# Decay blocks by a subtraction on GpSimd and one exponential, and two more gate blocks by seven products in the front

## The chip, the core and the metric

The kernel runs on one core of a Trainium2 chip. A core has a matrix engine (TensorE, PE in the profile; its weight loads are the row PEld), a vector engine (VectorE, DVE), a scalar engine for functions such as the exponential (ScalarE, ACT), GpSimd (POOL) and a sync engine (SP) that here issues nearly all DMA transfers. Each engine has its own instructions, in the order in which the program was written, and waits on semaphores for the others. The metric is the time of one execution on the device in microseconds (us).

## What is computed

One layer of a decoder on 1024 tokens of width 1024, in float32. One wide projection feeds two token mixers, and gates merge them:

```python
h = rms_norm(x, norm_w)
q, k, v, z_a, xbc, z_s, dt_raw, gate_logits = split(h @ w_in)
y_a = diff_attention(q, k, v) * silu(z_a)            # 8 heads, two softmax maps each
y_s = ssd_chunked(conv(xbc), softplus(dt_raw + dt_bias), -exp(a_log))   # 32 heads, 4 groups
y_s = gated_group_rms_norm(y_s, z_s)
merged = sigmoid(g_a) * (y_a @ w_proj_attn) + sigmoid(g_s) * (y_s @ w_proj_ssd)
out = x + merged @ w_out
```

The gate logits have 2048 columns, 16 blocks of 128: blocks 0 to 7 are g_a, 8 to 15 are g_s. In the chunked scan (8 chunks of 128 tokens) the decay of a head within a chunk is

```python
seg = a_t[..., :, None] - a_t[..., None, :]          # a_t: cumulative sum of dt * A in the chunk
decay = exp(where(causal, seg, -inf))                # 128 x 128 for each head
```

and multiplies the products of C and B before they meet x.

## The kernel before, in words

**Three-part products.** Float32 factors are split into a rounded high part and the rest, and a product is three matmuls: high by high, high by rest, rest by high (`steps3`). `hH` and `hL` are the two parts of h, 16 slices of 128 x 1024 together.

**Two ways for a block of the projection.** Directly, a block of 128 output columns is two halves of 512 tokens, each 8 row blocks of three matmuls (`gates`, `proj_half`): 48 matmuls of 512 columns. Or two neighbouring blocks, four quarters of a product, go together by seven products instead of eight (Strassen-like, `front_pair`): each of the seven takes a sum or difference of weight quarters (`pair_splits`, sums on GpSimd) and a form of h, which is a quarter or a sum of quarters of it. That is 7 x 4 x 3 = 84 matmuls for the pair, with additions behind them (`front_sum`, `gate_step`). The forms t1 to t4 of h are kept in 16 big buffers while the front lasts (`form_tiles`).

**Stages.** `bulk` writes TensorE's main stream, in this order:

1. the front: `FRONT_ORDER`, a list written out by hand. `y` and `e` are the first products of the z columns and of gate blocks 0, 2, 4 and 6 before all forms are there; `c` is a pair of convolution blocks, `g` a pair of gate blocks, `z06` and the like one of seven products of the z columns, `d` the dt columns. `FRONT` is 12: the front does gate blocks 0 to 11;
2. the eight attention heads' projections (`att_proj`, tile `pma`);
3. `gates`: the gate blocks from `FRONT` to 15, directly (tile `pg`). The second half of block 15 is the last use of h and frees its slices one by one for other data;
4. `products(0)`, `products(1)`, `products(2)`: the products of the two branches with their projections, each by seven products in two passes over pairs of output blocks (tiles `px`, `py`, `pz`); then `final`, the output product.

**What runs between.** Scan chunks (`ssd_core`, `ssd_chunk`), attention blocks (`att_core`, `att_block`), the sums of forms (`sums_of`), the loads and splits of forms for the products (`fill`, `get_form`) and those of weights (`w_loads`, `w_splits`) are tasks. While the program is built, a planner (`Plan`) keeps a clock for each engine with a cost for each instruction, and puts a task's next instructions into the stream when their inputs are due; otherwise the main stream goes on. So the order on every engine is fixed when the kernel is built; on the chip only the waits decide.

**Buffers around the change.** Of the big pool (17 buffers of 4 KB a partition) the forms of h hold 16 during the front. In the heads a head holds 4 (`v`, `zg`, two `kk`), a half of its queries 1, an attention block of the second half 2 (`p`), a decay block 1 (`abb`, one at a time). The products read forms too, 7 forms of 4 tiles for each of the three: `get_form` takes a slice pair of h if one is free, else a big buffer, and leaves three big buffers for others until attention and scan are done. A form is loaded, then copied on ACT and its rest taken on DVE (`split_form`). `products` uses the 28 tiles in the order `ORDER` in its first pass and gives them back in its second; b22 comes last in it.

**A decay block** (`load_ab`): the cumulative sums of 8 heads of a chunk are loaded to all partitions as 128 x 8 x 128, GpSimd's affine_select puts -1e30 where the key comes after the query, and ACT takes the exponential of each head's 128 x 128 with the bias `nac`, the negative cumulative sum of the partition: 8 instructions. Then DVE multiplies by `pc` (C times B), and TensorE uses the block in small matmuls (tiles `pD`, `pO`).

Of the kernel before, what the change touches and what calls it, by code (L numbers as in the profile page):

```python
# [11 lines left out]
AF = mybir.ActivationFunctionType  # L12
ALU = mybir.AluOpType
AX = mybir.AxisListType

P = 128
# [6 lines left out]
GH = 8  # L23
# [9 lines left out]
C_GATE = 9248  # L33
NBIG, NW, NRAW, NMID, NSM = 17, 9, 4, 16, 8
PACE = 17.5
FRONT = 12
SLOW = 32.0
FRONT_ORDER = "y0 e4 y1 e0 g8 c6 d0 c20 z06 c16 z07 c10 g0 c2 z05 z04 c0 z16 g6 z03 g2 z17 c4 z15 z13 z14 c8 c14 g4 c12 g10 c18 c22"
REST = (("t2", 6), ("b22", 3), ("t3", 7), ("t1", 5), ("t4", 4))
ZSUMS = (83.0, 185.0, 9.0)  # L40
WPOOL = 2
# [4 lines left out]
HOP = 0.12  # L46
# [107 lines left out]
def tile_hybrid_layer(ctx: ExitStack, tc: tile.TileContext, x, norm_w, w_in, q_norm_w, k_norm_w,  # L154
# [37 lines left out]
    def bigt(shape, dt=F32, name="b"):  # L192
        return big.tile(shape, dt, tag="b4", name=name)

    def midt(shape=(P, 512), dt=F32, name="m"):
        return mid.tile(list(shape), dt, tag="b2", name=name)
# [47 lines left out]
    def in_ps(*aps):  # L244
        return any(a.space == bass.MemoryType.PSUM for a in aps)
# [3 lines left out]
    def act(o, i, f, after, **kw):  # L249
        nc.scalar.activation(o, i, f, **kw)  # L250
        if f in (AF.Silu, AF.Exp) and f != table[0]:
            table[0] = f
            pl.op("A", 1.3, after)
        c = 0.83e-3 * i.free_size() + (0.052 if in_ps(i) else 0.093) + 0.093 * (("accum_out" in kw) + any(not isinstance(kw.get(i, 0.0), float) for i in ("scale", "bias")))
        return pl.op("A", c, after)

    def tt(o, a, b, op, after, eng="V"):
        (nc.vector if eng == "V" else nc.gpsimd).tensor_tensor(out=o, in0=a, in1=b, op=op)  # L258
        n = o.free_size()
        if eng == "G":  # L260
            return pl.op("G", 0.095 + (1.85e-3 if op == ALU.mult else 2.3e-3) * n, after, True)
        sb = not in_ps(a, b)
        return pl.op("V", 0.07 + 0.07 * sb + 1.042e-3 * n, after, sb)
# [14 lines left out]
    def load(o, i, after=0.0):  # L278
        nc.sync.dma_start(out=o, in_=i)
        q = pl.op("Q", 0.48, max(after, pl.t))  # L280
        n = o.free_size() * 512 / 360e3 if o.space != bass.MemoryType.DRAM else i.free_size() * 512 / 360e3
        return pl.op("D", n, q + 0.6) + lag[1]
# [83 lines left out]
    def block_w(src, nkb, c0, cols=P):  # L366
        return [(src[q * 512:(q + 1) * 512, c0:c0 + cols].rearrange("(k p) c -> p k c", p=P), 4, cols)
                for q in range(nkb // 4)]
# [5 lines left out]
    ORDER1 = []  # L374
    for e in FRONT_ORDER.split():
        ORDER1.append((e[0], int(e[1:])))
# [32 lines left out]
    NFRONT = len(wlist)  # L409
    for ob in range(FRONT, 16):  # L410
        wlist += block_w(w_in, KB, C_GATE + ob * P)
# [187 lines left out]
    def w_next(n):  # L599
        i = used[0]  # L600
        used[0] += n
        return list(range(i, i + n))
# [202 lines left out]
    def att_proj(h):  # L805
# [10 lines left out]
        for ts in ((0, 1), (2,), (3,), (4,), (5,), (6,), (7,)):  # L816
            pms = []
            for t in ts:
                k = yield from pl.get(trs, first=True)
                pms.append((mmt(f"pma{h}{t}"), k))  # L820
                if t % 2 == 0:
                    km = yield from pl.get(qkm)
                    qk.append([midt([P, 2, 256], name=f"qk{h}{t}"), km, 0])
            if FRONT == 16 and h == HEADS - 1 and ts[0] == NT - 1:
                pl.spawn(h_done())
# [12 lines left out]
    def h_done():  # L838
        yield pl.t + 5.6
        for k in range(2 * KB):  # L840
            hs.give(k, pl.t)
# [215 lines left out]
    nac = const.tile([P, NT, SH], F32, name="nac")  # L1057
# [435 lines left out]
    def ssd_core(g):  # L1493
        state = {"st": {}, "pre": {}, "n": 0, "did": set()}
        ssd_n[g] = state
        abs_ = {}

        def load_ab(c):
            k = yield from pl.get(abb)
            ab = bigt([P, GH, P], name=f"ab{g}{c}")  # L1500
            t = load(ab, act_d[c, g * GH:(g + 1) * GH, :].partition_broadcast(P)) + 1.0
            yield t
            nc.gpsimd.affine_select(out=ab, in_=ab, pattern=[[0, GH], [1, P]], compare_op=ALU.is_ge, fill=-1e30,  # L1503
                                    base=0, channel_multiplier=-1)
            t = pl.op("G", 1.06, t, True)
            yield t
            for j in range(GH):
                t = act(ab[:, j, :], ab[:, j, :], AF.Exp, t - HOP, bias=nac[:, c, g * GH + j:g * GH + j + 1])
            abs_[c] = (ab, k, t)
        need = [(b, h) for b in [16 + g, 20 + g] + list(range(g * 4, g * 4 + 4)) for h in range(2)]  # L1510
        while any(cv_at.get(i, INF) > pl.t for i in need) or any(z_at.get((g, t), INF) > pl.t for t in range(NT)):
            yield pl.t + 0.5
        pl.spawn(load_ab(0))
        for c in range(NT):
            if c + 1 < NT:
                pl.spawn(load_ab(c + 1))
            while c - state["n"] >= 2 or c and c - 1 not in state["did"]:
                yield pl.t + 0.2
            pl.spawn(ssd_chunk(g, c, state, abs_))
            yield pl.t + (PACE if bigs.avail(3) <= pl.t or 'setup' in ready else SLOW)  # L1520
# [181 lines left out]
    def gates():  # L1702
        for ob in range(FRONT, 16):
            ids = w_next(2)
            for n in range(2):
                k = yield from pl.get(trs, first=True)
                pm = mmt(f"pg{ob}{n}")
                yield from proj_half(pm, ids, n, n == 1, ob == 15 and n == 1)
                pl.spawn(gate_evac(ob, n, pm, k), pe_done())
# [541 lines left out]
```

## Time and profile before

| | us |
|---|---|
| median of 3 runs | 1552.48 |
| lowest, highest | 1551.68, 1552.88 |
| the profiled execution | 1552.03 |
| its span, first to last instruction | 1550.0 |
| first of the decay blocks' loads | 327.2 |
| last of the decay blocks' matmuls | 1069.6 |
| first, last matmul of the direct gate blocks (`pg`, 192) | 1179.6, 1236.6 |

How to read it: the page gives busy times and shares of the engines, the groups of instructions that cost most (mean ns of one, and the idle time of their engine before them), and the chain of waits that ended last, followed back from the end. The chain in order of time, the timeline and the windows show single stretches. Names such as `pg` are tiles of the program, written "out<-in". Ends of matmuls are modelled: one of 512 columns shows some 400 ns though the next begins about 227 ns after it, so starts are compared rather than lengths.

### The profile page before, as it was taken

Reading aid. Unit: us, or ns where it says so; the run is one execution under the profiler, and the core shown is the slowest. Engines: PE = TensorE matmul, PEld = TensorE weight load, DVE = VectorE, ACT = ScalarE, POOL = GpSimd, SP = SyncE. Lnnn points to the kernel's source line nnn. Section 1 sums busy time; section 2 is a strip of 40 time slices with the busy share of each in tenths; the row PEclk is TensorE's granted clock in tenths of the full one; section 3 lists DMA queues with packets and bytes.
Section 4 is the critical chain, followed back from the end, with each engine's and each line's share of the span. In section 5 each row is a group of like instructions: output and inputs, shape, how many; then the busy total and the mean of one; then the engine's idle time right before and its main releaser. Section 6 shows DMA issues by size and latency. Waiting matters only on the chain.

```text
span 1550.0 us, 26098 instructions
## 1 busy us (share of the span) xinstructions
PE 1534.9 (99%) x8562; PEld 1253.3 (81%) x8562; DVE 1131.5 (73%) x2091; ACT 887.6 (57%) x2203; POOL 806.9 (52%) x922
## 2 busy tenths in 40 slices
PE   7999999999999999999999999999999999999999
PEld 5887888888888878787878887888878888888887
DVE  6757978657688776877677777777456687888985
ACT  8654434355666666767766776766556555352350
POOL 3276376544555545455685645574768754322005
PEclk9999999999999999999999999999999999999999
DMA  7576678666544472324463424152438679698836
GB/s 237 172 222 215 218 254 292 205 200 224 187 143 130 133 215 77 117 77 143 153 204 117 150 76 135 62 174 82 157 137 264 228 275 315 227 333 262 308 130 224
DMA packets 255977, 289.56 MB, mean 187 GB/s; under 512 B 18519, under 2 KB 162656, under 8 KB 255842
## 3 DMA queue, kind: packets, MB, share of 16 engines
q1 hardware_dynamic: 255838, 287.89, 57.4%
q8 instruction: 68, 1.11, 0.3%
q14 instruction: 67, 0.55, 0.1%
q10 hardware_dynamic: 4, 0.00, 0.0%
HBM read 198.57 MB, written 89.26 MB: 186 GB/s over the span
## 4 chain that ended last, share of the span: by engine, by line
PE 91%; POOL 2%; DVE 2%; ACT 2%; DMA 2%; issue 1%; SPq 0%; POOLq 0%; DVEq 0%; ACTq 0%
PE pma L218 21%; PE pz L218 11%; PE fYc L218 6%; PE py L218 5%; PE fXc L218 4%; PE sc L218 4%; PE fZc L218 4%; PE av L218 4%; PE fYg L218 3%; PE px L218 3%; PE pO L218 3%; PE pg L218 3%; PE pmz L218 2%; PE pa L233 2%; PE poz L218 1%; PE fZg L218 1%
## 5 line engine op out<-in xcount | busy, mean ns | idle before, releaser
L218 PE MATMUL pma<-w,hH 128*128 128x512 f32 x1024 | 347.4, 407 | 0.6 <-ACT at L250 0.6
L218 PEld LDWEIGHTS pma<-w,hH 128*128 128x128 f32 x1024 | 186.9, 188 | 40.6 <-issue 5.5
L218 PE MATMUL pma<-w,hL 128*128 128x512 f32 x512 | 208.4, 407 | 0.0
L250 ACT ACTIVATE w<-raw 128x512 fp32r<-128x512 f32 (+1 forms) x166 | 102.5, 630 | 65.3 <-DMA raw<-wf_d 25.1
L218 PEld LDWEIGHTS pma<-w,hL 128*128 128x128 f32 x512 | 96.6, 189 | 20.0 <-issue 3.0
L258 POOL TENSOR_TENSOR rawf<-rawf,rawf 128x512 f32<-128x512 f32 x54 | 70.6, 1307 | 79.8 <-DVE wp L258 37.2
L258 DVE TENSOR_TENSOR w<-raw,w 128x512 fp32r<-128x512 f32 (+1 forms) x114 | 91.0, 810 | 23.8 <-ACT w L250 23.6
L250 ACT ACTIVATE p<-p,nm 128x256 f32<-128x256 f32 (+7 forms) x128 | 98.2, 769 | 17.1 <-DVE nm L946 13.8
L218 PE MATMUL fYc<-ft,wp 128*128 128x512 f32 x432 | 105.6, 391 | 0.0
L218 PEld LDWEIGHTS fYc<-ft,wp 128*128 128x128 f32 x432 | 80.6, 188 | 16.7
L258 POOL TENSOR_TENSOR w<-raw,w 128x512 fp32r<-128x512 f32 x52 | 69.9, 1350 | 41.2 <-ACT w L250 41.2
L218 PE MATMUL pz<-w,ft 128*128 128x512 f32 x384 | 91.3, 392 | 0.0
L250 ACT ACTIVATE wp<-rawp 128x512 fp32r<-128x512 f32 x72 | 44.5, 628 | 76.6 <-POOL rawp L258 18.2
L258 POOL TENSOR_TENSOR rawp<-rawp,rawp 128x512 f32<-128x512 f32 x36 | 52.7, 1469 | 59.8 <-DVE wp L258 50.8
L218 PEld LDWEIGHTS pz<-w,ft 128*128 128x128 f32 x384 | 71.5, 188 | 14.7
L250 ACT ACTIVATE ab<-ab,nac 128x128 f32<-128x128 f32 x256 | 78.4, 395 | 2.2 <-POOL ab L1503 1.7
L946 DVE CUSTOM_DVE_ANT_0 p<-sc,maskb 128x512 f32<-128x512 f32 (+3 forms) x128 | 69.1, 585 | 13.5 <-PE sc L218 13.3
L218 PEld LDWEIGHTS av<-v,at 128*128 128x128 f32 x576 | 73.3, 191 | 4.5 <-issue 0.4
L290 POOL TENSOR_TENSOR rs<-rs,mhalf 128x4 f32<-128x4 f32 (+1 forms) x71 | 73.1, 1030 | 5.9
L258 POOL TENSOR_TENSOR os<-os,os 128x512 f32<-128x512 f32 x48 | 68.9, 1436 | 13.4 <-DMA os<-in_w_in_dram 5.4
L218 PE MATMUL av<-v,at 128*128 128x128 f32 x576 | 75.4, 275 | 0.0
L250 ACT ACTIVATE wp<-rawf 128x512 fp32r<-128x512 f32 x100 | 60.1, 624 | 23.0 <-POOL rawf L258 20.6
(376 smaller groups left out, 4171.1 us busy)
## 6 DMA issues: line engine op xcount, KB each, us to landing
raw<-in_w_in_dram SPq DMA_DIRECT2D x104, 256.0 KB, 3.2
rawf<-in_w_in_dram SPq DMA_DIRECT2D x72, 256.0 KB, 3.8
ab<-act_d SPq DMA_DIRECT2D x32, 512.0 KB, 5.3
wf_d<-os SPq DMA_DIRECT2D x48, 256.0 KB, 2.3
cv_d<-cv SPq DMA_DIRECT2D x48, 256.0 KB, 2.5
raw<-wf_d SPq DMA_DIRECT2D x48, 256.0 KB, 3.2
t_d<-ts SPq DMA_DIRECT2D x24, 512.0 KB, 2.7
os<-in_w_in_dram SPq DMA_DIRECT2D x32, 256.0 KB, 5.2
```

What stands on the lines that cost most here:

```text
L218: nc.tensor.matmul(o, lhsT=lhsT, rhs=rhs, start=start, stop=stop, **kw)
L233: nc.tensor.transpose(out=o, in_=i, identity=ident if idn is None else idn)
L250: nc.scalar.activation(o, i, f, **kw)
L258: (nc.vector if eng == "V" else nc.gpsimd).tensor_tensor(out=o, in0=a, in1=b, op=op)
L290: nc.gpsimd.tensor_tensor(out=dst, in0=dst, in1=mhalf[:, 0:cols], op=ALU.pow)
L946: nc.vector.tensor_tensor_reduce(out=p[:, j:e], in0=sc[m][:, o:o + e - j], in1=maskb[:, S - n + j:S - n + e], scale=-1.0, scalar=nms[i - 1 ...
```

## The change

Three things are changed. Gate blocks 12 and 13 move from the direct way behind the heads to a pair by seven products in the front (`FRONT` 14, `g12` in the list); `gates` keeps blocks 14 and 15. The front's list has a new order: `z07` stands before `c16`, `c14` where `c4` was and `c4` behind `z15`, and `g12` behind `c12`. And in a decay block GpSimd adds `nac` to all eight heads at once, with `nac` repeated along the columns, and one exponential on ACT takes the whole block. That is the subtraction of the reference's `seg`, as `nac` is negative. The cost that the planner puts down for both is that of its helpers `tt` and `act`.

```diff
-FRONT = 12
+FRONT = 14
 SLOW = 32.0
-FRONT_ORDER = "y0 e4 y1 e0 g8 c6 d0 c20 z06 c16 z07 c10 g0 c2 z05 z04 c0 z16 g6 z03 g2 z17 c4 z15 z13 z14 c8 c14 g4 c12 g10 c18 c22"
+FRONT_ORDER = "y0 e4 y1 e0 g8 c6 d0 c20 z06 z07 c16 c10 g0 c2 z05 z04 c0 z16 g6 z03 g2 z17 c14 z15 c4 z13 z14 c8 g4 c12 g12 g10 c18 c22"
...
             t = pl.op("G", 1.06, t, True)
             yield t
-            for j in range(GH):
-                t = act(ab[:, j, :], ab[:, j, :], AF.Exp, t - HOP, bias=nac[:, c, g * GH + j:g * GH + j + 1])
+            t = tt(ab, ab, nac[:, c, g * GH:g * GH + GH].unsqueeze(2).to_broadcast([P, GH, P]), ALU.add, t, "G")
+            yield t
+            t = act(ab, ab, AF.Exp, t)
             abs_[c] = (ab, k, t)
```

## Prediction

> **What bounds the kernel now.** The page first: its busy shares, then the chain that ended last.
>
> ```profile
> PE 1534.9 (99%) x8562; PEld 1253.3 (81%) x8562; DVE 1131.5 (73%) x2091; ACT 887.6 (57%) x2203; POOL 806.9 (52%) x922
> PE 91%; POOL 2%; DVE 2%; ACT 2%; DMA 2%; issue 1%; SPq 0%; POOLq 0%; DVEq 0%; ACTq 0%
> ```
>
> TensorE is busy for 99% of the span and is 91% of the chain; nothing else passes 81%, and that is the weight load beside it. So an edit counts only where it changes TensorE's own work or makes it wait. Next the windows, cut at the stages (front; eight heads; tail of the last head; products). The columns are length, then busy time and count of PE, PEld, DVE, ACT and POOL, granted clock, DMA share and GB/s.
>
> ```profile
> 38.00:553.00 515.00, 515.00 (x2500) 422.87 (x2500) 377.83 (x600) 274.91 (x534) 272.15 (x219) 1.00 0.63 200
> 553.00:1179.60 626.60, 623.78 (x4243) 506.57 (x4241) 435.68 (x1011) 419.90 (x1308) 380.73 (x565) 1.00 0.41 130
> 1179.60:1273.20 93.60, 93.60 (x480) 76.88 (x479) 67.33 (x102) 53.81 (x118) 61.74 (x55) 1.00 0.83 277
> 1273.20:1534.00 260.80, 260.38 (x1148) 214.91 (x1147) 219.33 (x330) 108.17 (x190) 68.74 (x48) 1.00 0.76 255
> ```
>
> From 38 to 1534 us TensorE is idle for 1496 - 1492.76 = 3.2 us, 2.8 of it in the heads. Relieving another engine can win no more than that. Last I read the chain in order of time where the direct gate blocks stand, with the sync queue's timeline beside it.
>
> **Gate blocks 12 and 13.** One row of the chain in the front, then rows of it from the tail (start, length, what):
>
> ```profile
> 104.46 2.72 PE fZg L218 x12
> ```
>
> ```profile
> 1179.81 7.75 PE pg L218 x34
> ...
> 1195.43 1.18 PE sc L218 x12
> ...
> 1231.11 1.59 PE sc L218 x9
> ...
> 1272.69 5.44 PE pz L218 x24
> ```
>
> A matmul of 512 columns costs 2.72 / 12 = 0.2267 us in this stream. A direct block is 2 halves x 8 row blocks x 3 partial products = 48 matmuls; two blocks are 96, or 21.76 us, removed from between the heads and the products. The pair by seven products is 7 x 4 x 3 = 84, or 19.04 us, added to the front. TensorE's own work falls by **2.72 us**. That is the whole direct gain.
>
> Around it the pair needs 7 weight splits where the two blocks had 4, four sums of weights on GpSimd, and a copy and six additions behind the products. Its loads are 1 MB either way; four loads and four stores on the sync queue move to the front with it. All this lies beside the front's other products: there TensorE is busy for 515.00 of 515.00 us, while DVE has 137 us free, ACT 240 and POOL 243. I cost it at nothing; without the cover one late split would hold TensorE for about one product, 2.72 us. The swaps in the front (z07 before c16, c14 in the place of c4, c4 behind z15) move equal products about and I cost them at nothing too: the other products of the front fill the place.
>
> **What the removed 21.76 us covered.** Here I expect the time to be lost. The first branch product uses 7 x 4 = 28 tiles of forms in its first pass, and they stay until its second. The sync queue's timeline has their loads:
>
> ```profile
> 1177.06 1.93 SPq L279 DMA_DIRECT2D f0b<-ys_d  x4
> ...
> 1193.85 0.64 SPq L279 DMA_DIRECT2D f0b<-ys_d  x1
> ...
> 1228.05 0.32 SPq L279 DMA_DIRECT2D hH<-ys_d  x1
> ...
> 1243.39 0.32 SPq L279 DMA_DIRECT2D hL<-ys_d  x1
> ...
> 1261.55 1.21 SPq L279 DMA_DIRECT2D f0b<-ys_d  x2
> ```
>
> Nine (first and last row shown) go into big buffers by 1194 us. Sixteen (1228.05 to 1243.39, again first and last) go into h, which the last gate block frees. The last three, all for b22 (two in the last row), need big buffers again, and the last head's attention has those: 4 for the head, 1 for q, 2 for a block; with 9 forms that is 16 of its 17. So its last four blocks go one at a time (sc from 1195.43 to 1231.11, on average 11.9 us apart), and the last two loads come when the head lets go. What leads up to that, on POOL, DVE and ACT:
>
> ```profile
> 1253.41 0.88 POOL L290 TENSOR_TENSOR f<-f,mhalf 128x1 f32<-128x1 f32 x1
> ```
>
> ```profile
> 1202.22 0.68 DVE L258 TENSOR_TENSOR f0b<-f0b 128x512 fp32r<-128x512 f32 x1
> ...
> 1257.81 0.34 DVE L266 SCALAR_TENSOR_TENSOR y<-av,f,zg 128x128 f32<-128x128 f32 x1
> ...
> 1269.34 2.06 DVE L258 TENSOR_TENSOR f0b<-f0b 128x512 fp32r<-128x512 f32 x2
> ```
>
> ```profile
> 1266.84 1.28 ACT L250 ACTIVATE f0b<-f0b 128x512 fp32r<-128x512 f32 x2 [4.05 <-DMA f0b<-ys_d]
> ```
>
> The last b22 form is split at 1269.34 + 2.06 = 1271.40 us; TensorE wants it for its tenth matmul there, at 1272.69 + 9 x 0.2267 = 1274.73. The slack is **3.3 us**. The change takes 21.76 us of TensorE work out of just this interval, which opens where the heads end (1179.6). The attention tail can't move forward in it: its last block needs the last projection, and its blocks go one by one. So TensorE would wait up to 21.76 - 3.3 = 18.4 us. Queued behind that wait are all the products and the output, and the order is fixed.
>
> Some of it comes back, because less runs beside the end of the tail. The result y waited for DVE from 1254.29 (f done) to 1257.81: 3.5 us. The loads stood behind others from 1258.15 to 1261.55: 3.4 us. The split waited for DVE from 1268.12 to 1269.34 and took 0.7 us longer than two of 0.68: 1.9 us. If all 8.8 us go, 9.6 us are left. So the bounds are 9.6 and 18.4. I take the loads' and the split's 5.3 us as saved and leave y's delay, since weight splits still run on DVE there: **13.1 us**.
>
> A long wait may also cost clock (third column from the end, two windows that answer to gaps):
>
> ```profile
> 15.00:20.00 5.00, 3.06 (x14) 2.46 (x14) 2.97 (x6) 4.98 (x9) 1.53 (x4) 1.00 1.03 412
> 1545.00:1550.00 5.00, 1.22 (x8) 1.01 (x8) 0.85 (x2) 0.00 (x0) 0.00 (x0) 0.85 0.22 78
> ```
>
> With 1.9 us idle of 5 the clock stayed at 1.00; with 3.8 us idle it fell to 0.85. So the cost here lies between 0 and 0.15 x 5 = 0.75 us; I take 0, as attention's own matmuls break up the wait, and keep 0.75 for the range. The Trainium skill ("TensorE: Matmul & The Clock Gate", Part 1) states that an idle window of about 3.4 us halves the clock and that it takes about as long a busy one to restore it; as an estimate by that page the wait would cost 1.7 us more, and the sum would be 1564. By that rule the low clock of the last window is the idle end of the span, which the trace agrees with (0.85).
>
> **Decay blocks.** Groups by form (count, busy us, mean ns):
>
> ```profile
> L250 ACT ACTIVATE ab<-ab,nac 128x128 f32<-128x128 f32 x256 | 78.4, 395 | 2.2 <-POOL ab L1503 1.7
> ...
> L258 POOL TENSOR_TENSOR os<-os,os 128x512 f32<-128x512 f32 x48 | 68.9, 1436 | 13.4 <-DMA os<-in_w_in_dram 5.4 <-DMA hL<-ys_d 4.7 <-DMA os<-in_w_out_dram 1.0
> ...
> L258 POOL TENSOR_TENSOR xdt<-xn,dtt 128x512 f32<-128x512 f32 x32 | 36.2, 1131 | 68.8 <-ACT xn L250 68.8
> ...
> L250 ACT ACTIVATE p<-p,nm 128x1024 f32<-128x1024 f32 x16 | 18.4, 1153 | 0.0
> ```
>
> The eight exponentials of a block take 78.4 / 32 = 2.45 us on ACT. One of 1024 columns takes at most p's 1.15 us, which has the bias and a sum besides, and at least one short one's 0.40; nearest is p's, I take 1.1. ACT loses 32 x 1.35 = 43 us. The addition over 1024 columns isn't in the trace: 2 x 1.131 = 2.3 us by the broadcast product, 2 x 1.436 = 2.9 by the full one. I take 2.6, between them: POOL gains 32 x 2.6 = 83 us. A block's decay comes 2.6 + 1.1 - 2.45 = 1.25 us later.
>
> None of it is on TensorE. ACT's saving hides behind TensorE's 99%. POOL's 83 us, even if all fell into the heads, raise it from 380.73 to 464 of 626.6 us, 74%. The exponential now waits for POOL; behind it in ACT's queue stand copies of PSUM tiles, behind the addition in POOL's queue the roots and powers of attention, each up to 2.6 us later. They feed attention blocks, and the projections fill TensorE meanwhile. I take 0; the bounds are -2.8 us (all idle time of the heads goes) and +2.8 (it doubles).
>
> **Sum.** The profiled execution took 1552.03 us, 2.03 around its span; the median is 0.45 higher. 1552.03 - 2.72 + 13.1 + 0 = 1562.4, by the median 1562.9: I say **1562.5**. Its own range is 1552.03 - 2.72 + 9.6 - 2.8 = 1556.1 to 1552.03 - 2.72 + 18.4 + 0.75 + 2.8 = 1571.3.
>
> **Rivals.**
>
> *The cover holds* (not slower): the tail of attention with its loads shrinks to the shorter cover. From 1179.6 to the last split it takes 91.8 us; the need stands at 1274.73 - 1179.6 = 95.1 us, and will at 95.1 - 21.76 = 73.4. From a tail of 73.4 us on this decides. For it: four blocks 11.9 us apart are mostly waits between engines, which another order could shorten, and 8.8 us at the end are queueing. Against it: POOL's sums of output weights and the weight splits of the first product stay, and come into the same tail sooner. Time: 1552.48 - 2.72 = 1549.8.
>
> *GpSimd eats the gain*: cover holds, but the later decays and roots double the idle time of the heads, and 1549.8 + 2.8 = 1552.6. The Trainium skill ("GPSIMD Engine Reference", Key points) states that GpSimd shares its SBUF interfaces with VectorE and contends with its instructions of two SBUF inputs; no row quoted here has that price by itself.
>
> *Idle time goes*: cover holds and ACT's 43 us remove the heads' idle time: 1549.8 - 2.8 = 1547.0.
>
> **How the numbers follow.** A measurement of this kernel can tell about 0.2%, 3.1 us, from no change: bounds 1549.4 and 1555.6. Forecast 0.62 (all slower); cover holds 0.22, astride the lower bound, so half of it faster; GpSimd eats the gain 0.10 (same); idle time goes 0.06 (faster). Faster 0.11 + 0.06 = 0.17, same 0.11 + 0.10 = 0.21, slower 0.62. The cases lie on both sides: the likeliest one's own range is 1556 to 1571; the 8-in-10 range goes from 1548, which leaves out the last rival and little of the first, to 1570.
>
> **What would show it.** *Work*: 84 more matmuls in the front, 96 in the gate stage for 192. *Wait*: an idle gap of TensorE of 10 to 18 us in the seventh form of the first branch product, at pz, released by a split or a load of f0b; the loads of f0b still follow the last y. If TensorE is busy throughout there, my main step is wrong, and the loads show whether the tail got shorter or the buffers came from elsewhere. *Decay*: 32 additions of 2.3 to 2.9 us on POOL, 32 exponentials near 1.1 us, and idle time of the heads within 2.8 us of 2.8. If that grows by more, GpSimd is the cause to look for.

## The result, and the profile after

The changed kernel takes 1572.27 us (median of 3 runs, 1572.13 to 1574.37) against 1552.48: a ratio of 1.0128, with a 95% interval of 1.0111 to 1.0145. It is slower, 19.8 us by the medians and 20.3 by the profiled spans (1570.3 against 1550.0). The forecast was 1562.5 with a range up to 1570: the direction was right, but the 10.0 us forecast are half of what was lost, and the time lies above the range.

The page of the changed kernel, busy shares and chain:

```profile
PE 1542.3 (98%) x8550; PEld 1252.9 (80%) x8550; DVE 1149.4 (73%) x2098; ACT 848.6 (54%) x1985; POOL 873.0 (56%) x959
...
PE 95%; DMA 1%; POOL 1%; DVE 1%; ACT 1%; issue 1%; SPq 0%; DVEq 0%; POOLq 0%; ACTq 0%
```

ACT lost 39 us and POOL gained 66, as the change says. But TensorE, which had 12 matmuls less to do (2.72 us), is 7.4 us busier than before, and idle for 28.0 us where it was 15.1. So a wait is to be looked for also where TensorE counts as busy: a matmul of 512 columns shows 390 ns or more, while the next can begin 227 ns after it, and a shorter pause than the difference isn't seen as idle. Lengths of stages are the safer measure. The windows of the changed kernel (front; heads; from there to the end of b22 in the first branch product; the rest):

```profile
38.00:581.70 543.70, 541.65 (x2649) 444.02 (x2649) 394.84 (x620) 281.11 (x513) 304.32 (x241) 1.00 0.62 200
581.70:1209.83 628.13, 622.35 (x4187) 502.79 (x4186) 436.34 (x1004) 381.94 (x1124) 416.24 (x582) 1.00 0.40 126
1209.83:1298.41 88.58, 81.01 (x404) 64.00 (x403) 72.29 (x107) 50.38 (x111) 57.38 (x50) 0.98 0.77 255
1298.41:1570.30 271.89, 267.80 (x1188) 220.90 (x1187) 220.35 (x330) 106.04 (x187) 80.16 (x56) 1.00 0.79 265
```

And those of the kernel before, cut at the same two events of the tail:

```profile
1179.53:1278.13 98.60, 98.60 (x502) 81.03 (x501) 72.27 (x110) 56.27 (x123) 62.99 (x56) 1.00 0.80 269
1278.13:1550.00 271.87, 267.57 (x1189) 221.01 (x1187) 219.40 (x330) 105.77 (x185) 76.23 (x54) 1.00 0.77 256
```

The account follows from the boundaries:

- The heads end at 1209.83 instead of 1179.53, 30.3 us later. The pair put 19.04 us into the front. **11.3 us** are lost before the end of the heads, where the prediction put nothing.
- From there to the end of b22 it takes 88.58 us instead of 98.60. With 21.76 us of work taken away it should be 76.84. **11.7 us** are lost: the cover. (The expectations below say 11.8.)
- From there to the end 271.89 against 271.87: nothing.

Sum: -2.72 + 11.3 + 11.7 = 20.3, the difference of the spans.

The loss of the cover stands where it was predicted, at the seventh form. The chain of waits of the changed kernel in order of time (start, length, what), from the end of the form before b22:

```profile
1278.82 0.12 PE pya L233
...
1281.87 0.26 DVE y L266
1282.13 1.20 DVE p L266
...
1283.38 0.67 PE pa L233 x4
...
1284.72 3.44 PE av L218 x16
...
1288.19 0.37 ACT y L250 x2
1288.56 0.53 ACT f0b L250
...
1289.11 0.41 DVE f0b L258
...
1293.12 1.78 DVE f0b L258
1294.89 0.04 issue
1294.94 3.47 PE pz L218 x14
```

From 1278.82 to 1294.94 TensorE has little of its own to do: attention's last blocks go hand to hand between DVE, PE and ACT, then the forms of b22 are split, and the rest of b22's product can go. TensorE's waits for these results, over the whole span (us in all, times, longest):

```profile
PE pya L233 <- DVE y L266: 3.9, 2, 3.4
PE pa L233 <- DVE p L266: 0.8, 1, 0.8
PE pz L218 <- DVE f0b L258: 2.3, 4, 0.7
PE pz L218 <- ACT f0b L250: 1.0, 1, 1.0
```

So it is not one gap of 10 to 18 us at `pz`, as was forecast. About 4.2 us of idle time stand before matmuls of attention itself and 3.3 before `pz`. The last loads come late, and there are four of them now, not three (sync queue):

```profile
1279.93 0.93 SPq L279 DMA_DIRECT2D f0b<-ys_d  x2
1281.38 0.96 SPq L279 DMA_DIRECT2D f0b<-ys_d  x2
```

But they don't end the wait: they are issued before the last `y` (DVE, 1289.72), and a load of `f0b` lands 4.3 to 5.0 us after its issue. ScalarE copies the first two only at 1288.45, because its `y` of attention stands ahead of them in its order. Whether a free buffer or the queue held the loads is not shown; the first goes out right behind a store that had waited for VectorE until 1279.55. And VectorE's last three splits run beside three sums on GpSimd:

```profile
1289.42 4.91 POOL L258 TENSOR_TENSOR os<-os,os 128x512 f32<-128x512 f32 x3
```

```profile
1289.98 4.91 DVE L258 TENSOR_TENSOR f0b<-f0b 128x512 fp32r<-128x512 f32 x3
```

Alone such a split takes 0.68 us. Here each of the three ends some 0.55 us after the end of the sum that ran when it began, and together the four splits take about 3 us longer than 4 x 0.68.

Of the new pieces, by form:

```profile
L258 POOL TENSOR_TENSOR ab<-ab,nac 128x1024 f32<-128x1024 f32 x32 | 61.4, 1918 | 0.8
```

```profile
L250 ACT ACTIVATE ab<-ab 128x1024 f32<-128x1024 f32 x32 | 33.9, 1060 | 12.1 <-POOL ab L258 12.1
```

The exponential takes 1.06 us (estimated 1.1), the addition 1.92 (estimated 2.6, and below the lower bound of 2.3).

### The profile page after: what moved, and what is told of

It reads as the page before. It is cut to its first block, busy times and chain, and to the rows that moved or that the text cites. A ratio compares the mean times of both kernels' runs of the same rounds, so it can differ in the third digit from the quotient of the medians.

```text
span 1570.3 us, 25934 instructions
## 1 busy us (share of the span) xinstructions
PE 1542.3 (98%) x8550; PEld 1252.9 (80%) x8550; DVE 1149.4 (73%) x2098; ACT 848.6 (54%) x1985; POOL 873.0 (56%) x959
## 4 chain that ended last, share of the span: by engine, by line
PE 95%; DMA 1%; POOL 1%; DVE 1%; ACT 1%; issue 1%; SPq 0%; DVEq 0%; POOLq 0%; ACTq 0%
PE pma L218 23%; PE pz L218 10%; PE py L218 6%; PE fYc L218 6%; PE fZc L218 4%; PE sc L218 4%; PE av L218 4%; PE fXc L218 4%; PE px L218 4%; PE fYg L218 4%; PE pO L218 3%; PE pmz L218 3%; PE pa L233 2%; PE fZg L218 2%; PE fXg L218 2%; PE pg L218 1%
## 5 line engine op out<-in xcount | busy, mean ns | idle before, releaser
L218 PE MATMUL pma<-w,hH 128*128 128x512 f32 x1024 | 343.9, 406 | 0.0
L258 POOL TENSOR_TENSOR rawf<-rawf,rawf 128x512 f32<-128x512 f32 x57 | 74.9, 1314 | 63.6 <-DVE wp L258 29.3
L946 DVE CUSTOM_DVE_ANT_0 p<-sc,maskb 128x512 f32<-128x512 f32 (+3 forms) x128 | 69.1, 585 | 14.4 <-PE sc L218 14.1
L250 ACT ACTIVATE wp<-rawf 128x512 fp32r<-128x512 f32 x106 | 64.0, 624 | 28.8 <-POOL rawf L258 22.9
L258 POOL TENSOR_TENSOR os<-os,os 128x512 f32<-128x512 f32 x48 | 67.6, 1409 | 15.1 <-DMA wf_d<-os 9.0
L218 PE MATMUL sc<-kk,q 64*128 64x512 f32 (+3 forms) x576 | 70.4, 366 | 0.0
```

The costliest lines, as they stand in the source:

```text
L218: nc.tensor.matmul(o, lhsT=lhsT, rhs=rhs, start=start, stop=stop, **kw)
L946: nc.vector.tensor_tensor_reduce(out=p[:, j:e], in0=sc[m][:, o:o + e - j], in1=maskb[:, S - n + j:S - n + e], scale=-1.0, scalar=nms[i - 1 ...
```

## The experiments

Times are medians; the ratios are to the kernel before, run beside it on the same chip, so they are what is compared between experiments. One unit in the third place is 1.55 us.

### The parts one by one

The decay blocks alone, then the front alone (14 gate blocks and the new list, old decay), the pair alone (14 blocks, old list with `g12` put in), and the new list alone (12 blocks, without `g12`):

```diff
 e1_decay_only:  the hunk at load_ab of the change; FRONT 12, old list
 e2_front_only:  FRONT 14, the new list; load_ab as before
 e3_pair_only:   FRONT 14, the old list with g12 between c12 and g10
 e4_order_only:  FRONT 12, the new list without g12
```

> The kernel before with the new decay blocks alone. The changed kernel lost 11.2 us up to the end of the heads beyond its matmul count, and 11.8 us in a wait at b22. If GpSimd's additions cost the first of these: 8 to 11 us slower than before (1560 to 1564 us), with idle time of TensorE in the heads near 6 us, next to waits on GpSimd, and no wait at b22. If they cost nothing, as the prediction put it: within 3 us of 1552.5. If any new plan of the order loses some us wherever it falls: 2 to 6 us slower, in places that have nothing to do with GpSimd.

> The kernel before with FRONT 14 and the new list alone, decay as before. If the loss of cover is the cause of the wait at b22: the wait is here too, 10 to 14 us, and the time is -2.7 + 11.8 = 9.1 us above before (1560 to 1564 us). If the wait came from the later decay blocks or from GpSimd's load: no wait, 1550 us.

> The kernel before with FRONT 14 and g12 put into the old list, the other products of the front as before, decay as before. Loss of cover: as with the new list, 1560 to 1564 us with the wait at b22. If the new list is what costs, this one is nearer 1550.

> The kernel before with the new list without g12 (FRONT 12), decay as before: the same products in another order. Loss of cover and GpSimd both say within 2 us of 1552.5. If the list itself costs, 3 to 8 us slower, in the front. It also shows how far a mere new plan moves the time.

| | us | ratio | 95% |
|---|---|---|---|
| e1, decay | 1573.4 | 1.0132 | 1.0117 to 1.0147 |
| e2, front | 1581.4 | 1.0183 | 1.0168 to 1.0199 |
| e3, pair | 1586.0 | 1.0212 | 1.0195 to 1.0229 |
| e4, list | 1559.8 | 1.0046 | 1.0031 to 1.0061 |

e1, e2 and e3 are slower than every case that their expectations had; e4 is where the cost of the list was expected. Each part is slower by itself, and the parts don't add: decay (+20) and front (+28) together give +20. The decay blocks alone, which I had costed at nothing, are as slow as the whole change. By the boundaries above, the loss before the end of the heads is 23.8 us in e1, 7.3 in e4, 4.3 in e2 and 11.3 in the changed kernel: there the new decay blocks cost 7.0 us on top of the front. The loss at the cover is 26.9 us in e2; with the decay blocks added it is 11.7. So the price of the cover depends on the order too. In e3 it is 13.3 us, and 14.4 more are lost behind b22.

In e1 the heads take no longer than before (625.1 us); the first head's projection starts at 578.2 us, 23.5 later than the 554.7 of before, and the loss is in the front. TensorE is idle for 12.5 us from 38 us to there, where it was never idle before; the rest is not seen as idle time. The window of e1:

```profile
38.00:578.20 540.20, 527.66 (x2568) 431.65 (x2567) 399.82 (x617) 276.88 (x504) 296.19 (x233) 0.99 0.61 196
```

The largest wait there, in TensorE's timeline of e1 (in brackets the idle time before the instruction and its releaser):

```profile
546.86 0.39 PE L218 MATMUL fXc<-hH,wp 128*128 128x512 f32 x1
554.22 1.98 PE L218 MATMUL pO<-xdt,ab 128*64 128x64 f32 x32 [6.97 <-DVE ab L258]
```

and what DVE did meanwhile, in the chain of e1:

```profile
547.78 1.40 DVE cv L266 x2
549.18 1.25 DVE w L258
550.43 0.61 DVE pS L258
551.04 1.30 DVE cv L266 x2
552.35 0.60 DVE sl L258
552.94 1.14 DVE ab L258
```

The scan's matmul `pO` stands in TensorE's stream ahead of the front's products, and the product it needs stands in DVE's stream behind convolution steps. Both orders were written when the kernel was built; the front's next products (`fXc`) had run up to 546.86 and go on at 556.12, but stand behind `pO`.

### Same instructions, another order; same order, other instructions

The planner books costs, and these decide the order. So order and instructions can be exchanged: e5 books the addition and the single exponential of e1 and issues the eight exponentials of before; e6 books those eight and issues the addition and one exponential.

```diff
 e5_new_order_old_decay (against e1):
-            t = tt(ab, ab, nac[:, c, g * GH:g * GH + GH].unsqueeze(2).to_broadcast([P, GH, P]), ALU.add, t, "G")
+            t = pl.op("G", 0.095 + 2.3e-3 * GH * P, t, True)
             yield t
-            t = act(ab, ab, AF.Exp, t)
+            for j in range(GH):
+                nc.scalar.activation(ab[:, j, :], ab[:, j, :], AF.Exp, bias=nac[:, c, g * GH + j:g * GH + j + 1])
+            t = pl.op("A", 0.83e-3 * GH * P + 0.093, t)
 e6_old_order_new_decay (against before):
+            nc.gpsimd.tensor_tensor(out=ab, in0=ab, in1=nac[:, c, g * GH:g * GH + GH].unsqueeze(2).to_broadcast([P, GH, P]), op=ALU.add)
+            nc.scalar.activation(ab, ab, AF.Exp)
             for j in range(GH):
-                t = act(ab[:, j, :], ab[:, j, :], AF.Exp, t - HOP, bias=nac[:, c, g * GH + j:g * GH + j + 1])
+                t = pl.op("A", 0.83e-3 * P + 0.186, t - HOP)
```

> The order of e1_decay_only on every engine (the planner books the addition and the single exponential), but the eight exponentials of before are issued and GpSimd adds nothing. If GpSimd's 1.9 us additions held e1 up: near before, 1552 to 1558 us. If the new order of all the rest did it: as e1, 1569 to 1577 us, with TensorE idle in the front by about 12 us.

> The order of before on every engine (the planner books the eight exponentials), but the addition is issued on GpSimd behind the mask and one exponential on ACT in the place of the eight. If the additions cost time in themselves: 1560 us or more. If only the order costs: 1550 to 1555 us, as before, idle time of TensorE in the front 0 and in the heads 2 to 5 us.

e5 took 1573.4 us, ratio 1.0131 (1.0109 to 1.0153): all of e1's loss, without one addition. e6 took 1570.1, 1.0103 (1.0086 to 1.0121): most of it, with the order of before. So the edit can cost by either of two ways, and they don't add: e1, which has both, is no slower than e5. In e5 the waits of TensorE name the place again:

```profile
PE pO L218 <- DVE ab L258: 10.3, 5, 7.3
```

10.3 us in five waits for the same product, the longest 7.3, though no addition runs. In e6 it is the heads that grow, where before they took 624.83 us:

```profile
557.40:1197.73 640.33, 627.49 (x4235) 506.88 (x4233) 436.55 (x1007) 385.73 (x1131) 427.96 (x589) 0.99 0.40 126
```

### The cover put back

The changed kernel, with `gates` starting from block 12 again: blocks 12 and 13 are computed twice, and 96 matmuls stand behind the heads as before.

```diff
-    for ob in range(FRONT, 16):
+    for ob in range(12, 16):
...
-        for ob in range(FRONT, 16):
+        for ob in range(12, 16):
```

> The changed kernel, which computes gate blocks 12 and 13 a second time, directly, behind the heads: 96 matmuls, 21.8 us of TensorE, more than the changed kernel. If the wait at b22 is a matter of cover: the wait of 11.8 us goes, and the time is 1572.3 + 21.8 - 11.8 = 1582 us. If the wait has another cause (buffers held longer, loads later): it stays, and the time is 1594 us.

1582.0 us, ratio 1.018 (1.0164 to 1.0195). 21.76 us of work added cost 9.8 us by the medians and 8.1 by the ratios, so 12.0 to 13.7 of them run in time that was lost. From the end of the heads to the end of b22 it is 98.6 us again, as before, where the changed kernel has 88.4: by this 11.6 us. The window of e7, 62 us from the first matmul that reads `f0b`:

```profile
1269.70:1331.70 62.00, 62.00 (x274) 51.35 (x275) 54.28 (x67) 34.45 (x63) 26.71 (x18) 1.00 0.87 298
```

No idle time, clock 1.00. The same 62 us of the changed kernel, and of e2, which also lacks the cover:

```profile
1236.00:1298.00 62.00, 54.43 (x269) 42.52 (x268) 52.03 (x78) 33.93 (x78) 37.23 (x35) 0.97 0.71 233
```

```profile
1227.30:1289.30 62.00, 47.64 (x242) 38.49 (x241) 43.49 (x76) 31.24 (x72) 34.24 (x34) 0.94 0.62 206
```

7.6 and 14.4 us idle, at a lower clock; in e2 the stage goes on to 1306.5, with 18.7 us idle in all. The loss of the cover is shown from both sides.

### Is it the planner's cost of the addition, or the order as such?

The planner books 2.45 us for an addition that takes 1.92. e8 is e1 with 1.9 booked. e9 is the changed kernel's order with the eight exponentials of before and no addition (the edit of e5). e10 is the changed kernel without the pair: new list without `g12`, 12 blocks, new decay. e11 is the kernel before with 1.16 instead of 1.06 us booked for the mask: the same instructions, another order.

```diff
 e8_decay_booked_1p9 (against e1):
-            t = tt(ab, ab, nac[:, c, g * GH:g * GH + GH].unsqueeze(2).to_broadcast([P, GH, P]), ALU.add, t, "G")
+            nc.gpsimd.tensor_tensor(out=ab, in0=ab, in1=nac[:, c, g * GH:g * GH + GH].unsqueeze(2).to_broadcast([P, GH, P]), op=ALU.add)
+            t = pl.op("G", 1.9, t, True)
 e11_mask_booked_1p16 (against before):
-            t = pl.op("G", 1.06, t, True)
+            t = pl.op("G", 1.16, t, True)
```

> The kernel before with the new decay, as e1, but the planner books 1.90 us for the addition, what the trace shows, where its own rule gives 2.45. If a wrong cost in the plan is what spoils e1's order: 1549 to 1556 us. If any new order that was not picked out among many loses some: 1556 to 1575 us, with other waits than e1.

> The order of the changed kernel on every engine, with the eight exponentials of before in the place of the one and no addition on GpSimd. If the changed kernel's waits in the heads (5.8 us idle, the longest stretch at 880 to 902 us behind GpSimd) come from the additions' time: 1564 to 1568 us, idle time in the heads near 2 us, and the wait at b22 as before. If the order alone makes them: within 2 us of 1572.

> The changed kernel without the pair: new list without g12, FRONT 12, new decay. Loss of cover: the pair costs -2.7 + 11.8 = 9.1 us, so this is at 1563 us, with no wait at b22. If the pair is a gain in this list, it is at 1575 us.

> The kernel before; the planner books 1.16 us for the mask on GpSimd in place of 1.06 (the trace shows a mean of 1.16). No instruction is added, removed or changed; only the order in which tasks are put into the streams comes out otherwise. If only the change's own parts cost: 1552 us, within 2. If the order of before is one picked out among many, and any other costs: 5 to 20 us slower, with waits in the front or the heads.

| | us | ratio | 95% |
|---|---|---|---|
| e8, addition booked at 1.9 | 1567.5 | 1.0089 | 1.0072 to 1.0105 |
| e9, order after, old decay | 1575.7 | 1.0141 | 1.0126 to 1.0156 |
| e10, new list and decay, no pair | 1573.7 | 1.0131 | 1.0114 to 1.0148 |
| e11, mask booked at 1.16 | 1557.0 | 1.0022 | 1.0013 to 1.0031 |

e9 settles that in the changed kernel the additions with the single exponentials cost nothing against the eight exponentials: with the old instructions it is no faster, and it loses 11.6 us before the end of the heads. The order alone makes the loss. e8's better cost gives some 7 us back, not 20. e10 missed its 1563: it has the cover again, but its heads end 17.8 us later than before without the pair's work, where the changed kernel lost 11.3. In e11 nothing but a number of the planner differs, 0.1 us more for each of 32 masks, and the kernel is 3.4 us slower, between the two cases expected. With the instructions of before, every other order tried was slower, by 3.4 (e11), 7 (e4) and 20 us (e5).

### What an addition costs in the order of before

e6 left open why. e12 is e6 without the addition (the decay lacks the subtraction). e13 puts in its place, on GpSimd, two powers of a small tile of their own that nobody waits for (the subtraction is left out again). e14 moves the addition to VectorE. e15 is e6 with the exponential issued up to 2.3 us of the plan's time later, behind ScalarE instructions that come due meanwhile; every other engine's order is the same.

```diff
 e12_old_order_no_add (against e6):
-            nc.gpsimd.tensor_tensor(out=ab, in0=ab, in1=nac[:, c, g * GH:g * GH + GH].unsqueeze(2).to_broadcast([P, GH, P]), op=ALU.add)
 e13_pow_beside (against e12):
+            for n in (4, 3):
+                nc.gpsimd.tensor_tensor(out=dum[:, 0:n], in0=dum[:, 0:n], in1=mhalf[:, 0:n], op=ALU.pow)
 e14_add_on_vector (against e6):
-            nc.gpsimd.tensor_tensor(out=ab, in0=ab, in1=nac[:, c, g * GH:g * GH + GH].unsqueeze(2).to_broadcast([P, GH, P]), op=ALU.add)
+            nc.vector.tensor_tensor(out=ab, in0=ab, in1=nac[:, c, g * GH:g * GH + GH].unsqueeze(2).to_broadcast([P, GH, P]), op=ALU.add)
 e15_exp_later (against e6):
-            nc.scalar.activation(ab, ab, AF.Exp)
+            t0 = t
...
+            yield t0 + 2.3
+            nc.scalar.activation(ab, ab, AF.Exp)
```

> The order of before, as e6_old_order_new_decay, one exponential for the block, but the addition is left out (the decay lacks its subtraction), so GpSimd does no more than before. If the additions cost e6 its 17 us: 1549 to 1554 us. If the single exponential (it ends later for the first heads, 1.06 us against eight steps) or the changed waits do: 1560 us or more.

> The order of before and one exponential per block, as in the run without additions (1551.6), and in GpSimd's queue, where the additions stood, two powers of a small tile of their own (4 and 3 columns, about 1.1 + 0.9 = 2.0 us, as long as an addition); nobody waits for them, and the decay lacks the subtraction. If the additions cost 18 us because GpSimd's queue is later for attention's roots and powers: about 1570. If they cost it because the decay block itself comes later (mask, addition, exponential one behind the other): about 1552.

> The order of before, one exponential per block, and the addition on VectorE instead of GpSimd, about 1.2 us each (its product over the same 1024 columns takes 1.21): GpSimd is as before. If what counts is GpSimd's queue alone: within 3 us of 1552. If in this fixed order any queue that attention needs is as tight, VectorE with 73% above all: 12 us over before or more, about 1564 (0.65 of the 18, as 1.2 us is of 1.9).

> The run with the order of before and the new decay (1570.1), with one difference: the exponential is issued up to 2.3 us of the plan's time later, behind the ScalarE instructions that come due meanwhile; the order on every other engine is the same. If ScalarE's queue, standing before the exponential until the addition is done (65.6 us in all there; 35.6 with the addition on VectorE, which lost 10 us), is what costs the 18 us: that wait falls below 20 us, and at 0.27 us lost per us of it the time is about 1552 to 1557. If it is the later decay block itself: no better than 1570.

| | us | ratio | 95% | ACT before the exponentials waits |
|---|---|---|---|---|
| e12, no addition | 1551.6 | 0.9987 | 0.9977 to 0.9996 | 1.2 |
| e13, powers beside | 1554.4 | 1.0007 | 0.9997 to 1.0016 | 0.9 |
| e14, on VectorE | 1561.8 | 1.0051 | 1.0034 to 1.0068 | 35.6 |
| e15, exponential later | 1559.7 | 1.0052 | 1.0033 to 1.0071 | 24.5 |
| e6 | 1570.1 | 1.0103 | 1.0086 to 1.0121 | 65.6 |

The last column is the tile's view of `ab`, in us. Its rows of e6, e14 and e15, what ended the idle time of the exponential's engine (us, times):

```profile
  POOL ab L1507: 65.6, 27
```

```profile
  DVE ab L1507: 35.6, 26
```

```profile
  POOL ab L1507: 24.5, 13
```

e13 had 1.03 + 0.86 = 1.9 us of powers for each block on GpSimd, as long as an addition, and lost 3 us against e12: GpSimd's time by itself is nearly free. Nor do the additions slow VectorE much. It is busy for 1134.0 us in e6 and 1131.3 in e12. Of its 256 splits of 128x512 between buffers (`w`, `wp`, `f0b`), 60 take over 0.8 us in e6 and 65 in e12, and only two of the 60 began while an addition ran. What costs is ScalarE standing before the exponential. It takes its instructions in order; 27 of 32 times the addition isn't done when the exponential's turn comes, and attention's copies stand behind it. The loss against e12 (difference of the ratios times 1552.5) is 18.0 us in e6 for 65.6 us of that wait and 9.9 in e14 for 35.6: 0.27 and 0.28 us for each. (e14 was expected at 12 us or more.) e15 takes 41 us of the wait away and 7.9 of the 18 us with it. Its number was missed (expected 1552 to 1557): the wait stayed at 24.5 and not under 20, and at 0.27 that would be 6.6 us, where 10.1 were measured, each of these differences being known to some 3 us. So ScalarE's place in its order is shown to be a large part, by taking 41 of the 65.6 us away; that the rest of the loss is the rest of that wait, and not the later decay block, is only argued from the proportion.

Of the versions that compute the whole reference none ran faster than the kernel before.

## Why the prediction was wrong, step by step

- **The matmuls.** 12 fewer (8562 to 8550), 84 into the front, 96 out of the gate stage: right.
- **The cover**, taken at 13.1 us with bounds of 9.6 and 18.4: right in place, and near in size, 11.7 measured, 11.6 to 13.7 by e7. "Cover holds" (0.22) fell: from the end of the heads to the last split the tail needed 1294.90 - 1209.83 = 85.1 us, 6.7 less than the 91.8 of before, where 73.4 were needed. The last links were not the forecast ones. The loads didn't follow the last `y`; what came last was attention's own chain, and then ScalarE's and VectorE's place in their orders. I took the split's delay as saved, and GpSimd's sums made it longer. So the nearness of 13.1 and 11.7 is in part luck: the same cover cost 26.9 us in the order of e2.
- **The clock**, taken at nothing with 0.75 as the upper bound: too low. In the changed kernel the granted clock of the stage is 0.98 over 88.58 us, some 1.8 us (two decimals, so 1.3 to 2.2). It is in the 11.7. The chain shows it directly: behind an idle time of 3.35 us and one of 0.80, 16 matmuls `av` take 3.44 us, where 16 took 1.78 in the kernel before (at 1249.91). The Trainium skill ("TensorE: Matmul & The Clock Gate", Part 1), by which the wait would cost 1.7 us more, was nearer than the bound from the last window of the span; as a forecast it was made for one long wait, so that agreement tests its rule only roughly.
- **The swaps in the front at nothing**: wrong. e4, the list alone, is 7 us slower, 3.3 of it idle time in the front.
- **Three terms at nothing: decay blocks (within 2.8 us), swaps, and what surrounds the pair in the front.** This is the step that failed, with one reason for all three: that other products fill TensorE meanwhile. I read "TensorE is 99% busy, so POOL's and ACT's time hides behind it" from busy shares, and took the bounds from the 2.8 us of idle time in the heads. That holds for an engine's time (e13: 60 us more on GpSimd, 3 us lost) and not for its place in a fixed order. In place of nothing the changed kernel loses 11.3 us before the end of the heads, and e9 shows that its order alone does it. Alone the decay edit costs 20 us, by either of two ways: in the order of before, ScalarE stands before the exponential (e6); with the costs booked, the whole order is another, and the scan's products come late in the front (e1, e5). In the changed kernel it was the second: ScalarE waited 12.1 us there, and e9 without additions is no faster. I had looked at what queues behind the exponential and priced it at "up to 2.6 us later" each, then set it to nothing because projections fill TensorE; but TensorE's order is fixed too, and it fills nothing that isn't next in its stream. How the 11.3 us divide is known only in part: e2, the front alone, loses 4.3 there, and the decay blocks added to it 7.0, in one order of each.
- **"GpSimd eats the gain"** fell as a mechanism: not GpSimd's load (56%) but the order. The idle time of the heads grew to 5.8 us, just past the 5.6 from which the prediction would look to GpSimd; e9, without additions, has 6.4. **"Idle time goes"** fell: e12, with the exponential alone and no addition, gains 2.0 us (0.6 to 3.6 by its interval).
- The sum, 1562.4, lacked 11.3 us before the end of the heads and had 1.4 too many in the wait: 1562.4 + 11.3 - 1.4 = 1572.3; the profiled execution took 1572.13.

What stays open is why just the order of before fits so well. e11 shows how little moves it, and where e1 and e5 wait is seen, but not which of the planner's choices leads there; nor why decay, list and pair together lose 11.3 us up to the end of the heads, while decay and list without the pair lose 17.8; nor why the cover costs 26.9 us in e2 and 11.7 with the decay blocks added.

## What to carry to other kernels

Where the order on every engine is fixed when the kernel is built, the cost of an edit isn't the time it adds to an engine with room, but how far it moves an instruction that others stand behind: look at what follows the waiting instruction in its queue, and take no bound from the idle time there is. An edit that changes a planner's costs is first of all a new order; build it once with the new costs and the old instructions, and once the other way, before the edit itself is judged. And before work is taken from a stage, ask what waits it covers: here 21.76 us of matmuls hid 11.7 us of attention's tail. The rows of before named the place and a size near it; in another order of the same stage the price was more than double.

## What the runs showed of the hardware

An addition on GpSimd with one operand repeated along the columns is cheaper than with two full ones: 1.92 us for 1024 columns, where two full operands of 512 take 1.31 (`rawf`) to 1.49 (`rawp`) in the changed kernel. Powers of only 4 and 3 columns take 1.03 and 0.86 us (e13). One exponential over 1024 columns takes 1.06 us against 8 x 0.31 for eight with a bias, and the 44 us that ScalarE gains by it were worth 2.0 us (e12).

VectorE can stand still for GpSimd. Its split of 128x512 between two buffers takes 0.68 us. In the changed kernel 62 of 258 such splits (`w`, `wp`, `f0b`, each a subtraction) took over 0.8 us, up to 1.85; 60 of these began while a GpSimd instruction ran, and all 60 ended 0.54 to 0.56 us after that instruction's end. In all the 62 took some 44 us more than at 0.68. It isn't every time: 36 others began while GpSimd ran and were not slowed.
